# Phase tables of a state-space layer in quarters, one of them kept in DRAM for a while, and one unit moved two places in the order

## The chip, the cores and the metric

The kernel runs on one core of a Trainium2 chip. The metric is the device time of one execution in microseconds, as the median of several executions. The core has TensorE (matmuls; its weight loads are listed apart), VectorE (DVE in the rows), ScalarE (ACT), GpSimd (POOL) and SyncE (SP), which sends most DMAs here. Each engine works through its own queue in order.

## The reference

One step of a decoder layer with two parallel branches, for 1024 prompt tokens and 8 x 4 sample tokens. An RMSNorm feeds one input projection; its columns go to differential attention (four heads, a gate) and to a diagonal complex state-space layer (32 groups of 16 channels, 64 states each, a GLU, a gate); one output projection leads back to the residual stream. The part that the change touches is the state-space layer:

```python
dt = exp(log_dt); mag = exp(a_re * dt)
abar = mag * (cos(a_im * dt) + 1j * sin(a_im * dt))
bbar = ((abar - 1) / a) * b
h[l] = abar * h[l-1] + bbar @ u[l]          # per group, 64 complex states
y = Re(c @ h) + d * u
z = gelu(y); z = z * sigmoid(z @ w_glu + b_glu)
out_ssm = z * silu(gs)
```

## The kernel before

The state-space layer and the first attention head's projection come first (`first_phase`, up to about 262 us of the profiled execution); attention, the other heads and the output projection follow. In the first phase the 1024 tokens are cut into 128 chunks of 8 tokens (`NK`, `CH`). The 16 pairs of groups are handled in four *maps* m = 0 to 3 of four pairs each. For a map:

- `ssm_maps` (unit M) forms the products W (six VectorE products of 128x512, lines 573 to 578) and G (GpSimd, lines 734 and 736, three passes over 128x1152) in the tiles W, Wt and G. It also builds the block-diagonal bd and scales C on ScalarE.
- `ssm_kernel` (unit N) transposes W on TensorE into BT and multiplies G by bd into the chunk's kernel, which goes through DRAM into MT.
- `norm_u` (unit L) scales the chunk inputs U by the tokens' inverse RMS, after `u_store` (unit U) has turned them through DRAM.
- `ssm_states` (unit S) multiplies U by BT, copies the result into St (ScalarE, line 786; one buffer), rotates it by the phase table E (lines 792 to 797, VectorE and GpSimd), scans over the chunks (lines 801 and 802, VectorE), rotates back into H (lines 806 to 813).
- `ssm_out` (unit O) adds MT times U and G times H on TensorE and applies the gelu (line 837, ScalarE).

The rotation uses E = exp(i phase) for each state and chunk, tiles E_re and E_im. `phases` (unit P, line 683) makes them for *half* of the maps at a time (two maps, 8 x 128 phases per partition): on VectorE a copy, seven additions that double the filled part, the reduction to within half a turn (lines 689 to 695), then on ScalarE a sine, an absolute value and a second sine (lines 696 to 698). The two halves share one buffer each for E_re and E_im, so the second half (P1) is made only after the second map (S1) has used the first.

Statistics: the tokens' squares are summed on ScalarE (line 295), and `stats` (unit T, lines 314 to 322 with `rsqrt`, lines 176 to 183) makes inverse roots in eleven-odd small VectorE operations; the last that counts here writes `rr` (line 318). `chunk_roots` (unit R) spreads them by two matmuls, which head the queue of TensorE from then on; `spread` (unit D) stores the roots to DRAM (`xrd`, line 338) and reads them back to all partitions. The gate's weights (unit W, `stream_b`, line 214) are loaded by SP and split into a high and a low part (line 201 on ScalarE, line 204 on VectorE or GpSimd). Units C, G, J are matmul units: channel projections, twelve gate products, eighteen pieces of the first head. Unit V splits the first head's weights.

What sets the order: `UNITS` (line 47) is the order in which the units are written down. On TensorE that order is kept as it stands. The queues of the other engines, SP's among them, are ordered when the program is built, by a scheduler that takes an instruction when its inputs and buffers are free by its own estimates, and among several the one written first. At run time each queue is in order, and waits.

Buffers: tiles of one tag share a fixed number of buffers (G three, U, BT and MT two, St, X and H one, `big` with W, Wt, Z and others four). Before the maps start, `spare` lends such buffers to the twelve loads of the transposed input (`SPARE`, line 75); E_re and E_im are among those lent.

Of the kernel before, what the change touches and what calls it, by code (L numbers as in the profile page):

```python
# [9 lines left out]
F32 = mybir.dt.float32  # L10
# [3 lines left out]
OP = mybir.AluOpType  # L14
AX = mybir.AxisListType

D = 1024
# [8 lines left out]
W = 512  # L26
# [14 lines left out]
NK = S // CH  # L41
SPLITS = ((0, 352), (352, 352), (704, 352))
UC = 145
HC = 137
VW = 383

UNITS = ("M0 P0 T0 C20 C30 U0 U1 C21 R0 L0 M1 N0 C31 D0 S0 C22 L1 C32 U2 W X M2 N1 G G O0 S1 P1 L2 N2 G U3 G S2 O1 G L3 M3 G V0 N3 O2 G G S3 G V1 J J G G G Q0 J J O3 J Z0 J A0 J J B0 Z1 J Z2 J J J H0 Z3 J J H1 J J J H2 J Y0 H3 Y1 Y2 Y3").split()

GAP = 12
DUE = 5  # L50
# [21 lines left out]
NMORE = 2  # L72
LEAD = 4
PARTS = (256, 256, 512)
SPARE = {"xT": ("U", "U", "St", "H", "E_re", "E_im", "MT", "BT", "BT"),
         "xtok": ("St", "H", "BT", "BT", "MT", "MT")}
ORDER = ((0, 1, 2, 3, 4, 5, 6, 7, -1), (0, 1, 2, 3, 4, 5, -1, 6, 7))

# [65 lines left out]
class Kernel:  # L144
# [151 lines left out]

    def spare(self, name):

        sizes = {"U": (8 * UC, 2), "St": (8 * UC, 1), "H": (8 * HC, 1), "BT": (1024, 2), "MT": (1024, 2), "E_re": (8 * NK, 1),
                 "E_im": (8 * NK, 1)}  # L300
        n = self.spares.get(name, 0)
        tag = SPARE[name][n % len(SPARE[name])]
        self.spares[name] = n + 1
        return self.ss.tile([128, sizes[tag][0]], F32, name=name, tag=tag, bufs=sizes[tag][1])
# [48 lines left out]
    def first_phase(self):  # L353
        self.U, self.E, self.H, self.z_d, self.z, self.gz, self.glus = {}, {}, {}, {}, {}, {}, []
        self.zero = self.ss.tile([128, UC - NK], F32, name="zero")
        self.nc.gpsimd.memset(self.zero, 0.0)
        self.cn = self.p.tile([128, CN_W], F32, name="cn")
        nc = self.nc
        nc.sync.dma_start(self.cn, self.I["cn"])
        self.idn = self.cn[:, 0:128]  # L360
        self.A = [self.ap.tile([128, 2, NTOK], F32R, name="xt%d" % kt) for kt in range(KT)]
        self.xs = self.ap.tile([128, KT, 2, 32], F32R, name="xs")
        self.xv = self.p.tile([128, 9], F32, name="xv")
        nc.gpsimd.memset(self.xv, 1.0)
        self.spares = {}
        self.xT = []
        raw = []
        src = self.I["w_in"]
        self.sp = self.ss.tile([128, SP_W], F32, name="sp")
        for n, (n0, nn) in enumerate(SPLITS):  # L370
            parts = []
            for k0 in range(0, KT, 2):
                x = self.spare("xT")[:, 0:2 * nn].rearrange("p (k c) -> p k c", k=2)
                nc.sync.dma_start(x, self.I["xT"][128 * k0:128 * k0 + 256, n0:n0 + nn].rearrange("(k p) c -> p k c", k=2))
                parts.append((k0, 2, x))
                if n == 0 and k0 % 4 == 0:
                    i = k0 // 4
                    r = self.big("wraw")[:, 0:1024]
                    nc.sync.dma_start(r.rearrange("p (k c) -> p k c", k=4),
                                      src[512 * i:512 * i + 512, 2048:2304].rearrange("(k p) c -> p k c", k=4))  # L380
                    raw += [r[:, 0:512], r[:, 512:1024]]
            self.xT.append(parts)
            if n == 0:
                nc.sync.dma_start(self.sp, self.I["sp"])
        w = self.stream_b(2048, 1)
        self.turn = True
        self.uT = {}
        self.wu = []
        tc = self.tc
        for n in range(3):  # L390
            self.load_x(n)
            if n == 0:
                self.wu += [self.split_w(r) for r in raw]
                self.ssm_tables()
            for m in (0, 1):
                self.u_part(m, n)
        self.wu += list(w)
        for n in range(3):
            self.squares(n)
        self.gs_d = {}  # L400
        gs = None
        hs, self.w0 = self.first_head(), []
        unit = {"T": lambda i: self.stats(), "M": self.ssm_maps, "N": self.ssm_kernel, "D": lambda i: self.spread(), "R": lambda i: self.chunk_roots(), "U": self.u_store, "L": self.norm_u, "P": self.phases,
                "Z": self.load_z, "Q": lambda i: self.load_wglu(), "A": lambda i: self.lam(), "B": lambda i: self.bias(), "H": self.load_gz, "Y": self.glu, "S": self.ssm_states, "O": self.ssm_out}
        with tc.manual_schedule(engines={mybir.EngineType.PE}):
            for c in UNITS:
                if c[0] == "W":
                    self.turn = None
                    wg = list(self.stream_b(2560))
                elif c[0] == "X":  # L410
                    for kt in range(KT):
                        self.nc.scalar.activation(self.xs[:, kt, :, :], self.A[kt][:, :, S:NTOK].bitcast(F32), AF.Copy)
                    gs = self.gate(wg)
                elif c[0] == "C":
                    self.u_part(int(c[1]), int(c[2]))
                elif c[0] == "G":
                    next(gs)
                elif c[0] == "V":
                    self.turn = None
                    self.w0.append([self.split_w(r) for r in self.half_head(int(c[1]))])  # L420
                elif c[0] == "J":
                    next(hs)
                else:
                    unit[c[0]](int(c[1]))
            assert next(gs, None) is next(hs, None) is None
# [254 lines left out]
        f1, f2 = (ft[:, o:o + 128].rearrange("p (t b) -> p t b", t=16) for o in (0, 128))  # L680
        self.cmul(g, self.fins[:, 0], self.fins[:, 1], h_re, h_im, a4r, a4i, f1, f2)

    def phases(self, hf):
        nc, v, ss = self.nc, self.nc.vector, self.ss
        hs = slice(8 * hf, 8 * hf + 8)
        f = E_re = ss.tile([128, 8, NK], F32, name="E_re", tag="E_re", bufs=1)
        E_im = ss.tile([128, 8, NK], F32, name="E_im", tag="E_im", bufs=1)

        v.tensor_copy(f[:, :, 0], self.tw[:, 0, hs])
        for i in range(7):  # L690
            n = 1 << i
            v.tensor_tensor(f[:, :, n:2 * n], f[:, :, 0:n], self.tw[:, i, hs][:, :, None].to_broadcast([128, 8, n]), op=OP.add)
        magic = 1.5 * 2.0 ** 23
        v.tensor_scalar(E_im, f, magic, None, op0=OP.add)
        v.scalar_tensor_tensor(f, E_im, magic, f, op0=OP.subtract, op1=OP.subtract)
        nc.scalar.activation(E_im, f, AF.Sin, scale=-TURN)
        nc.scalar.activation(f, f, AF.Abs)
        nc.scalar.activation(E_re, f, AF.Sin, scale=-TURN, bias=self.quarter)
        self.E[hf] = E_re, E_im

    def sp_cols(self, name, m):
        a, b = SP[name]
# [68 lines left out]
    def ssm_states(self, m):  # L771
        nc, ss = self.nc, self.ss
        v, g = nc.vector, nc.gpsimd
        ts = slice(4 * m, 4 * m + 4)
        col = lambda name: self.sp_cols(name, m)
        U = self.U[m]
        G, BT, MT = self.maps[m]
        St = ss.tile([128, 2, 4, UC], F32, name="St", tag="St", bufs=1)
        for r in range(2):
            for th in range(2):  # L780
                q = (self.sc, self.tr)[th]()
                for tl in range(2):
                    t = 2 * th + tl
# [1 line left out]
                        self.mm(q[64 * g2:64 * g2 + 64, UC * tl:UC * tl + UC], BT[:, 2 * t + g2, r, :], U[:, 2 * t + g2, :], True, True)  # L785
                nc.scalar.activation(St[:, r, 2 * th:2 * th + 2, :], q[:, 0:2 * UC].rearrange("p (t k) -> p t k", t=2), AF.Copy)

        e4 = slice(4 * (m % 2), 4 * (m % 2) + 4)
        er, ei = (x[:, e4, :] for x in self.E[m // 2])
        sr, si = St[:, 0, :, 0:NK], St[:, 1, :, 0:NK]  # L790
        X = ss.tile([128, 3, 4, NK], F32, name="X", tag="X", bufs=1)
        v.tensor_tensor(X[:, 0], er, sr, op=OP.mult)
# [10 lines left out]
        H = ss.tile([128, 8, HC], F32, name="H", tag="H", bufs=1)  # L803
# [680 lines left out]
```

## Time and profile before

| | |
|---|---|
| median of 3 runs | 672.67 us (672.23 to 678.18) |
| the profiled execution | 677.08 us, its span 675.1 us |
| TensorE matmul busy in that span | 602.6 us (89%) |
| VectorE busy | 454.8 us (67%) |
| ScalarE busy | 320.1 us (47%) |
| GpSimd busy | 135.5 us (20%) |
| mean granted TensorE clock | 0.946 of full speed |

The rows that follow the change come from views of this one execution. Times are microseconds from the start of the span. A row of the timeline has the start, the time from the first start to the last end of instructions that were merged, engine, line of the program, operation, what is written from what, its shape and how many; in brackets the time that the engine sat idle before it and what ended that. A row of waits has the waiting engine, tile and line, the releaser, the total, the number and the longest. An engine that waits for a port inside an instruction counts as busy.

### The profile page before, as it was taken

To read this page: it belongs to the slowest core of one execution; us is meant where nothing else is said; L and a number is where in the kernel's file an instruction comes from. 1 tells how busy PE (TensorE), PEld (TensorE's weight loads), DVE (VectorE), ACT (ScalarE), POOL (GpSimd) and SP (SyncE) were. 2 spreads that over 40 slices of the span, in tenths; PEclk is the share of its full clock that TensorE was granted. 3 is DMA by queue.
4 is the path that set the end of the run, shared out by engine and by line. 5 is a ranking of instruction groups with operands and counts; after the bars stand their busy time and mean duration, and the time that the engine had idled before them with its cause. 6 is when DMAs were issued, how large, how long until landed. Compare 5 with 4: busy or idle time off the path is not lost.

```text
span 675.1 us, 11321 instructions
## 1 busy us (share of the span) xinstructions
PE 602.6 (89%) x3696; PEld 508.5 (75%) x3696; DVE 454.8 (67%) x1455; ACT 320.1 (47%) x798; POOL 135.5 (20%) x117
## 2 busy tenths in 40 slices
PE   5898867819999999897989999989999969999997
PEld 4897866819999989665757778767787748887775
DVE  5988968692624433787979899669876899832111
ACT  6893442613055333463747666556645566421000
POOL 0336785471412233000011000011000120001000
PEclk9997879859999999896999999999999988999999
DMA  9788553314155636433244300144100366233221
GB/s 308 255 214 151 134 149 97 118 52 133 54 179 167 192 106 193 146 102 103 70 127 122 88 24 25 48 120 138 39 25 17 88 199 202 89 105 125 82 84 50
DMA packets 90712, 79.65 MB, mean 118 GB/s; under 512 B 10365, under 2 KB 78558, under 8 KB 90654
## 3 DMA queue, kind: packets, MB, share of 16 engines
q1 hardware_dynamic: 85950, 72.36, 36.5%
q10 hardware_dynamic: 4704, 6.57, 2.7%
q8 instruction: 29, 0.48, 0.3%
q14 instruction: 29, 0.24, 0.1%
HBM read 56.70 MB, written 22.20 MB: 117 GB/s over the span
## 4 chain that ended last, share of the span: by engine, by line
PE 50%; DVE 27%; ACT 7%; issue 6%; DMA 6%; POOL 3%; SPq 1%; POOLq 0%; ACTq 0%; DVEq 0%
PE acc L152 33%; PE sc L152 7%; PE pv L152 4%; DVE s L1132 3%; PE tr L1157 2%; PE tr L152 2%; DVE ws L204 2%; DMA wraw<-in_w_in 2%; DVE qt L1017 1%; DVE qss L906 1%; DVE H L809 1%; DVE s L1142 1%; DVE qt L1016 1%; ACT ws L201 1%; DVE kt L1020 1%
## 5 line engine op out<-in xcount | busy, mean ns | idle before, releaser
L152 PE MATMUL acc<-ws,xt 128*128 128x512 f32 (+1 forms) x960 | 207.8, 359 | 0.0
L152 PEld LDWEIGHTS acc<-ws,xt 128*128 128x128 f32 x960 | 148.6, 190 | 19.9 <-issue 2.4
L204 POOL TENSOR_TENSOR ws<-wraw,ws 128x512 fp32r<-128x512 f32 x30 | 42.9, 1436 | 371.9 <-ACT ws L201 363.6
L152 PE MATMUL acc<-xt,ws 128*128 128x352 f32 x576 | 101.6, 337 | 10.0 <-ACT ws L201 7.9
L152 PEld LDWEIGHTS acc<-xt,ws 128*128 128x128 f32 x576 | 97.1, 198 | 13.3 <-ACT ws L201 8.4
L152 PE MATMUL acc<-ws,o 128*128 128x512 f32 x336 | 84.5, 400 | 1.5 <-ACT ws L201 0.9
L152 PEld LDWEIGHTS acc<-ws,o 128*128 128x128 f32 x336 | 63.0, 192 | 15.0 <-ACT ws L201 1.3
L152 PE MATMUL sc<-kt,qt 128*128 128x256 f32 (+1 forms) x320 | 58.4, 297 | 11.3 <-DVE mn L1132 5.8
L152 PEld LDWEIGHTS sc<-kt,qt 128*128 128x128 f32 x320 | 46.7, 192 | 26.2 <-DVE mn L1132 8.6
L1137 ACT ACTIVATE s<-s,mn 128x128 f32<-128x128 f32 (+7 forms) x64 | 49.5, 774 | 31.0 <-DVE mn L1132 24.9
L201 ACT ACTIVATE ws<-wraw 128x512 fp32r<-128x512 f32 x68 | 41.4, 626 | 39.6 <-PE acc L152 15.4
L204 DVE TENSOR_TENSOR ws<-wraw,ws 128x512 fp32r<-128x512 f32 x38 | 36.9, 980 | 31.8 <-ACT ws L201 31.5
L1366 DVE TENSOR_TENSOR xres<-acc,xres 128x512 f32<-128x512 f32 x16 | 11.0, 690 | 52.7 <-PE acc L152 52.7
L152 PE MATMUL pv<-vo,wt 128*128 128x128 f32 x288 | 41.0, 285 | 0.7 <-ACT wt L1160 0.6
L152 PEld LDWEIGHTS pv<-vo,wt 128*128 128x128 f32 x288 | 36.1, 194 | 6.2 <-ACT wt L1160 5.4
L1160 ACT ACTIVATE wt<-tr 128x512 f32<-128x512 f32 (+3 forms) x48 | 22.6, 487 | 17.3 <-PE tr L1157 17.1
L1132 DVE CUSTOM_DVE_ANT_0 s<-sc,cb 128x512 f32<-128x512 f32 (+3 forms) x48 | 26.6, 553 | 5.1 <-PE sc L152 4.8
L1142 DVE SCALAR_TENSOR_TENSOR s<-s,ls 128x128 f32<-128x128 f32 (+7 forms) x32 | 27.2, 849 | 0.3
L1157 PE MATMUL tr<-cn,s 128*128 128x128 f32 x144 | 25.2, 285 | 0.7 <-ACT ot L1196 0.3
L1132 DVE CUSTOM_DVE_ANT_0 s<-sc,TB,mn 128x256 f32<-128x256 f32 (+1 forms) x56 | 24.8, 442 | 0.8
L152 PE MATMUL acc<-z,ws 128*128 128x352 f32 x144 | 23.9, 325 | 1.3 <-DVE ho L462 1.0
L152 PEld LDWEIGHTS acc<-z,ws 128*128 128x128 f32 x144 | 23.1, 188 | 1.8 <-DVE ho L462 1.3
(296 smaller groups left out, 986.5 us busy)
## 6 DMA issues: line engine op xcount, KB each, us to landing
wraw<-in_w_in SPq DMA_DIRECT2D x36, 256.0 KB, 3.2
xT<-in_xT SPq DMA_DIRECT2D x12, 352.0 KB, 7.2
xtok<-in_x SPq DMA_DIRECT2D x8, 512.0 KB, 3.8
cached<-in_cache_k SPq DMA_DIRECT2D x64, 64.0 KB, 1.8
cached<-in_cache_v SPq DMA_DIRECT2D x64, 64.0 KB, 1.9
wraw<-in_w_out SPq DMA_DIRECT2D x16, 256.0 KB, 2.9
xres<-in_x SPq DMA_DIRECT2D x16, 256.0 KB, 3.0
out_y<-xres SPq DMA_DIRECT2D x16, 256.0 KB, 2.1
```

Source lines behind the costliest of these rows:

```text
L152: self.nc.tensor.matmul(out, lhsT, rhs, start=start, stop=stop)
L201: nc.scalar.activation(hi, raw, AF.Copy)
L204: (nc.vector if self.turn else nc.gpsimd).tensor_tensor(lo, raw, hi.bitcast(F32), op=OP.subtract)
L809: v.tensor_tensor(H[0:64, g2::2, 1:NK + 1], X[ps, 0], X[ps, 2], op=OP.subtract)
L906: v.tensor_reduce(ss[0:n, 4 * i:4 * i + 4], qn[0:n, i].rearrange("p (c d) -> p c d", d=QD), axis=AX.X, op=OP.add)
L1016: v.tensor_copy(hi[ot], hi[ps].bitcast(F32))
L1132: v.tensor_tensor_reduce(out=s[:, k0 + a0:k0 + a1], in0=q[:, a0:a1], in1=bias, op0=OP.add, op1=OP.min, scale=1.0, scalar=last, accum_out=m)
L1137: nc.scalar.activation(s[:, 0:L], s[:, 0:L], AF.Exp, bias=last, scale=-1.0, accum_out=ls[:, 2 * i + c:2 * i + c + 1])
L1142: v.scalar_tensor_tensor(wv, st[1][:, 0:L], cf, wv, op0=OP.mult, op1=OP.add)
L1157: nc.tensor.transpose(q[:, 128 * b:128 * b + 128], wv[:, 128 * (b0 + b):128 * (b0 + b) + 128], self.idn)
L1160: nc.scalar.activation(wt[:, 0:128 * bn], q[:, 0:128 * bn], AF.Copy)
L1366: v.tensor_tensor(x, a, x, op=OP.add)
```

## The change

The tables are made a map at a time (4 x 128 phases), with three buffers each for E_re and E_im instead of one of twice the size. All four are made at one place in front, in the order P0, P3, P1, P2, so that ScalarE needs no second stay in the sine's table. The one for map 3 is stored to DRAM as soon as it is made, which frees its buffers for the fourth that is made; a new unit E3, `phases_back`, written down right after S0, loads it back into the buffers that map 0 has left. The products of map 3 (M3) are written down after S1, where P1 stood, instead of after L3. The input's loads borrow two buffers of G instead of E_re and E_im.

```diff
-UNITS = ("M0 P0 T0 C20 C30 U0 U1 C21 R0 L0 M1 N0 C31 D0 S0 C22 L1 C32 U2 W X M2 N1 G G O0 S1 P1 L2 N2 G U3 G S2 O1 G L3 M3 G V0 N3 O2 G G S3 G V1 J J G ...
+UNITS = ("M0 P0 P3 P1 P2 T0 C20 C30 U0 U1 C21 R0 L0 M1 N0 C31 D0 S0 E3 C22 L1 C32 U2 W X M2 N1 G G O0 S1 M3 L2 N2 G U3 G S2 O1 G L3 G V0 N3 O2 G G S3 G V1 J J G ...
-SPARE = {"xT": ("U", "U", "St", "H", "E_re", "E_im", "MT", "BT", "BT"),
+SPARE = {"xT": ("U", "U", "St", "H", "G", "G", "MT", "BT", "BT"),
...
-    def phases(self, hf):
+    def phases(self, m):
         nc, v, ss = self.nc, self.nc.vector, self.ss
-        hs = slice(8 * hf, 8 * hf + 8)
-        f = E_re = ss.tile([128, 8, NK], F32, name="E_re", tag="E_re", bufs=1)
-        E_im = ss.tile([128, 8, NK], F32, name="E_im", tag="E_im", bufs=1)
+        hs = slice(4 * m, 4 * m + 4)
+        f = E_re = ss.tile([128, 4, NK], F32, name="E_re", tag="E_re", bufs=3)
+        E_im = ss.tile([128, 4, NK], F32, name="E_im", tag="E_im", bufs=3)
...
-            v.tensor_tensor(f[:, :, n:2 * n], f[:, :, 0:n], self.tw[:, i, hs][:, :, None].to_broadcast([128, 8, n]), op=OP.add)
+            v.tensor_tensor(f[:, :, n:2 * n], f[:, :, 0:n], self.tw[:, i, hs][:, :, None].to_broadcast([128, 4, n]), op=OP.add)
...
-        self.E[hf] = E_re, E_im
+        if m == 3:
+
+            self.e_d = self.dr.tile([2, 128, 4 * NK], F32, name="ed")
+            for i, x in enumerate((E_re, E_im)):
+                nc.sync.dma_start(self.e_d[i], x.rearrange("p t k -> p (t k)"))
+        else:
+            self.E[m] = E_re, E_im
+
+    def phases_back(self, m):
+        self.E[m] = []
+        for i, n in enumerate(("E_re", "E_im")):
+            x = self.ss.tile([128, 4, NK], F32, name=n, tag=n, bufs=3)
+            self.nc.sync.dma_start(x.rearrange("p t k -> p (t k)"), self.e_d[i])
+            self.E[m].append(x)
...
-        e4 = slice(4 * (m % 2), 4 * (m % 2) + 4)
-        er, ei = (x[:, e4, :] for x in self.E[m // 2])
+        er, ei = self.E[m]
```

## Rows read from the trace of the kernel before

**Rows 1.** Waits of TensorE from 28 to 180 us: total, times, longest.

```profile
PE tr L752 <- DVE W L575: 9.8, 1, 9.8
PE sc L152 <- ACT St L786: 4.4, 1, 4.4
PE tr L152 <- POOL G L736: 4.2, 1, 4.2
PE tr L152 <- DVE rr L318: 4.1, 1, 4.1
```

**Rows 2.** Busy time by stretch: from:to, length, engines, granted clock, DMA share, GB/s.

```profile
140.00:152.00 12.00, 3.17 (x24) 2.09 (x24) 11.49 (x10) 2.62 (x5) 8.38 (x5) 0.50 0.19 59
152.00:177.00 25.00, 24.96 (x188) 24.29 (x184) 11.59 (x22) 6.26 (x18) 5.53 (x7) 0.94 0.36 101
...
177.00:240.00 63.00, 61.99 (x490) 60.78 (x491) 26.46 (x31) 26.92 (x46) 19.78 (x13) 1.00 0.52 158
```

**Rows 3.** Timeline of GpSimd, first map's G: first and last of three.

```profile
44.81 2.27 POOL L734 TENSOR_TENSOR Wt<-C,P 128x1152 f32<-128x1152 f32 x1 [2.93 <-DMA C<-in_c]
...
49.40 2.64 POOL L736 TENSOR_TENSOR G<-G,Wt 128x1152 f32<-128x1152 f32 x1
```

**Rows 4.** Timeline of VectorE, first half of the tables and the statistics.

```profile
39.16 0.69 DVE L204 TENSOR_TENSOR ws<-wraw,ws 128x512 fp32r<-128x512 f32 x1 [1.38 <-ACT ws L201]
39.76 2.38 DVE L692 TENSOR_TENSOR E_re<-E_re,tw 128x8 f32<-128x8 f32 x7
42.18 0.70 DVE L694 TENSOR_SCALAR E_im<-E_re 128x1024 f32<-128x1024 f32 x1
42.91 1.22 DVE L695 SCALAR_TENSOR_TENSOR E_re<-E_im,E_re 128x1024 f32<-128x1024 f32 x1
45.78 1.33 DVE L314 TENSOR_SCALAR xv<-xv 128x9 f32<-128x9 f32 x1 [1.65 <-ACT xtok L295]
...
52.10 0.17 DVE L179 SCALAR_TENSOR_TENSOR xr<-xtmp,xr 128x9 f32<-128x9 f32 x1
...
53.13 0.29 DVE L318 TENSOR_TENSOR rr<-cn,xr 128x128 f32<-128x128 f32 x1
```

**Rows 5.** Timeline of VectorE, second half of the tables and after.

```profile
113.63 1.04 DVE L689 COPY E_re<-tw 128x8 f32<-128x8 f32 x1
...
119.50 1.23 DVE L695 SCALAR_TENSOR_TENSOR E_re<-E_im,E_re 128x1024 f32<-128x1024 f32 x1
...
126.75 0.69 DVE L792 TENSOR_TENSOR X<-E_re,St 128x512 f32<-128x512 f32 x1 [5.59 <-ACT E_re L698]
...
143.65 1.35 DVE L513 TENSOR_TENSOR U<-U,RU 128x1160 f32<-128x1160 f32 x1
```

**Rows 6.** Timeline of GpSimd, the last map's G: first and last pass.

```profile
120.82 2.26 POOL L734 TENSOR_TENSOR G<-C,P 128x1152 f32<-128x1152 f32 x1 [4.25 <-ACT C L730]
...
148.01 2.94 POOL L736 TENSOR_TENSOR G<-G,Wt 128x1152 f32<-128x1152 f32 x1
```

**Rows 7.** Timeline of ScalarE: weight splits, first states, second stay in the sine's table.

```profile
64.24 0.63 ACT L201 ACTIVATE ws<-wraw 128x512 fp32r<-128x512 f32 x1 [5.70 <-DMA wraw<-in_w_in]
...
67.94 0.46 ACT L786 ACTIVATE St<-sc 128x290 f32<-128x290 f32 x1
...
121.20 1.28 ACT L696 ACT_TABLE_LOAD   x1
122.50 1.06 ACT L696 ACTIVATE E_im<-E_re 128x1024 f32<-128x1024 f32 x1
```

**Rows 8.** Timeline of TensorE: the last of the first map's state products.

```profile
63.92 0.67 PE L152 MATMUL tr<-U,BT 128*64 128x145 f32 x8
```

**Rows 9.** Timeline of SP's queue: the roots' store and the gate's weights.

```profile
53.12 0.37 SPq L338 DMA_DIRECT2D xrd<-xr  x1
53.54 1.62 SPq L214 DMA_DIRECT2D wraw<-in_w_in  x3
```

**Rows 10.** DMA issues of the page: tile, queue, count, KB each, us to landing.

```profile
xtok<-in_x SPq DMA_DIRECT2D x8, 512.0 KB, 3.8
```

More of the change, by code (lines that the diff above doesn't have):

```diff
@@ L45 @@
 VW = 383
-UNITS = ("M0 P0 T0 C20 C30 U0 U1 C21 R0 L0 M1 N0 C31 D0 S0 C22 L1 C32 U2 W X M2 N1 G G O0 S1 P1 L2 N2 G U3 G S2 O1 G L3 M3 G V0 N3 O2 G G S3 G V1 J J G G G Q0 J J O3 J Z0 J A0 J J B0 Z1 J Z2 J J J H0 Z3 J J H1 J J J H2 J Y0 H3 Y1 Y2 Y3").split()
+UNITS = ("M0 P0 P3 P1 P2 T0 C20 C30 U0 U1 C21 R0 L0 M1 N0 C31 D0 S0 E3 C22 L1 C32 U2 W X M2 N1 G G O0 S1 M3 L2 N2 G U3 G S2 O1 G L3 G V0 N3 O2 G G S3 G V1 J J G G G Q0 J J O3 J Z0 J A0 J J B0 Z1 J Z2 J J J H0 Z3 J J H1 J J J H2 J Y0 H3 Y1 Y2 Y3").split()
 GAP = 12
@@ L297, in spare @@
     def spare(self, name):
-        sizes = {"U": (8 * UC, 2), "St": (8 * UC, 1), "H": (8 * HC, 1), "BT": (1024, 2), "MT": (1024, 2), "E_re": (8 * NK, 1),
-                 "E_im": (8 * NK, 1)}
+        sizes = {"U": (8 * UC, 2), "St": (8 * UC, 1), "H": (8 * HC, 1), "BT": (1024, 2), "MT": (1024, 2), "G": (1152, 3)}
         n = self.spares.get(name, 0)
@@ L402, in first_phase @@
         hs, self.w0 = self.first_head(), []
-        unit = {"T": lambda i: self.stats(), "M": self.ssm_maps, "N": self.ssm_kernel, "D": lambda i: self.spread(), "R": lambda i: self.chunk_roots(), "U": self.u_store, "L": self.norm_u, "P": self.phases,
+        unit = {"T": lambda i: self.stats(), "M": self.ssm_maps, "N": self.ssm_kernel, "D": lambda i: self.spread(), "R": lambda i: self.chunk_roots(), "U": self.u_store, "L": self.norm_u, "P": self.phases, "E": self.phases_back,
                 "Z": self.load_z, "Q": lambda i: self.load_wglu(), "A": lambda i: self.lam(), "B": lambda i: self.bias(), "H": self.load_gz, "Y": self.glu, "S": self.ssm_states, "O": self.ssm_out}
```

## Prediction, before the changed kernel was run

> **What bounds the kernel now.** I read the waits of TensorE first, since its order in this phase is written out by hand: an instruction there that is not ready holds all behind it. Between 28 and 180 us its four longest waits are for the last map's products (VectorE's W), for the copies of the second-last states, for GpSimd's G and for the token statistics (rr) [rows 1]. The table of busy time by stretch says what kind of place each is. From 140 to 152 us TensorE works 3.17 of 12 us while VectorE shows 11.49 and GpSimd 8.38; from 152 on it is full, 24.96 of 25 and 61.99 of 63 [rows 2]. So whatever brings forward the output products of the third map (O2, which begin at 152 us) should reach the end; whatever is won behind a wait that stays is lost.
>
> Two busy engines at 140 to 152 us would mean that one could still be relieved. The timeline denies it. GpSimd forms G in three back-to-back instructions from 44.81 to 52.04 [rows 3]; VectorE's statistics run beside them, and there the first operation on 128x9 numbers takes 1.33 us and ends at 47.11, where GpSimd's first pass ends, while such an operation after 52.04 takes 0.17 [rows 4]. VectorE and GpSimd take turns. So I laid their instructions on one line: from 37 to 152 us neither runs in only nine gaps, 6.1 us together, the first the 1.38 us ahead of the weight split at 39.16 [rows 4], the last and largest inside the 5.59 us wait at 126.75 [rows 5]. The bound up to 152 us is this pair, not either engine.
>
> The Trainium skill, SBUF — State Buffer, "Who interferes with whom", gives the rule: a VectorE instruction with two SBUF inputs contends with a GpSimd instruction that reads SBUF, and the loser "fully blocks". The trace agrees: 1.33 us beside 0.17. The rule speaks against this change: counted engine by engine, products made earlier would free TensorE's 9.8 and 4.2 us of waits, 14 in all and some 659 us; counted as a pair, moving them frees nothing by itself.
>
> **The change part by part.**
>
> *The second half of the tables leaves the middle.* It now runs on VectorE from 113.63 to 120.73 [rows 5]. Undisturbed, the first half cost 0.17 (its copy, as its neighbours) + 2.38 + 0.70 + 1.22 = 4.5 us [rows 4]; the rest of the later stretch is blocking and two gate operations. So 4.5 us of the pair's work goes. With it goes the wait for its sines, 5.59 us on VectorE [rows 5]. GpSimd fills part of it, with G until 123.08 [rows 6] and two small products; the last three of the nine gaps, 2.1 us, are what is left. Gain 6.6.
>
> *Table loads.* Two go, 1.28 us each [rows 7]. The first lies inside the 5.59 us just counted; the second stands before the output's gelu, behind which nothing of the pair waits: nothing more. The Trainium skill, ScalarE: Activation LUTs, "What ACT_TABLE_LOAD costs", puts a switch at 2.66 us, a drain of 1.38 included. Here the load begins at 121.20, takes 1.28, and the sine begins at 122.50 [rows 7]: no drain shows; with one, the gain would be 1.4 more.
>
> *The last map's products two places up.* Their work (six VectorE products, three GpSimd passes ending at 150.96 [rows 6]) is not less; it runs inside the scan chain of the second map, which it lengthens, and no longer behind that of the third. For the pair that is a swap, and O2 needs both. Two small terms remain. The scaling of the last U (1.35 us at 143.65 [rows 5]), which O2 does not need, may fall behind: 0 to 1.35, I take 1. And the third map's states are copied by ScalarE (four copies of some 0.46, as the first map's [rows 7]) only once the second map's chain has let go of their buffer; today the sines hide this. Two copies and their start come bare if the products are used up by then: 0 to 2.5, I take 1. What stands behind them in ScalarE's queue are the gate's tanh and weight splits, which have slack. These cancel.
>
> *Quarters in front.* The trace has no quarter. Its large operations halve, its small ones do not: 0.17 + (2.38 - 0.69 + 0.2) + 0.40 + 0.66, about 3.1 us, estimated from the half [rows 4]; the bounds are 2.2 (half of a half) and 4.5. Four make 12.4 where one half made 4.5: 7.9 us more for the pair between 37 and 70 us. VectorE's idle 1.38 and 1.65 us take 3.0 at most. In detail: VectorE has the port from 38.8 to 44.8, which the first two quarters fill (6.2). The third runs into GpSimd's G and gets through only at its ends; at 52.04 I leave it 2.3 us of work. The statistics stand behind it by the order list: eleven small operations, 2.2 us unblocked. rr then ends at 52.04 + 4.5 = 56.5 instead of 53.4 [rows 4]: 3.1 late. Behind rr wait TensorE's root products with all after them, and on SP's queue the store of the roots with the gate's weight loads. The fourth quarter must wait for a buffer, that of the quarter stored to DRAM; its 3.1 us fall among the second map's products, which have a few us of slack. The first scan chain starts 3.1 to 6.2 late; I take 3.6.
>
> *ScalarE, DMA, buffers.* Twelve sine and absolute passes of some 0.6 us (1.06 for twice the size [rows 7]) replace three of 1.06: 4 us more, in a stretch where ScalarE idles 5.70 us for weights [rows 7]. Store and reload are 0.5 MB each; a load of 512 KB lands in 3.8 us [rows 10]. The reload waits for the first quarter's last reader and is needed only by the fourth map; what it holds up on SP, second-half gate weights and the next map's C, is not near its use. The input's spare buffers move to G's: cover enough, since those are free until the first map.
>
> **The sum.** 6.6 + 1 - 1 - 3.6 = 3.0 us gained, before second-order shifts in the order of VectorE's and ScalarE's queues, which no row prices. The profiled execution took 677.08 (span 675.1), 4.4 above the median of 672.67; the sum is the same against either: 674.1, or **669.7** as a median. Bounds: best 6.6 + 1.35 - 0 - 0 = 8.0, or 664.7; worst 6.6 + 0 - 2.5 - 6.2 = -2.1, or 674.8.
>
> **Rivals.**
>
> *The front is hidden.* TensorE's first state products end at 64.6 [rows 8], but ScalarE copies them only from 67.94, behind weight splits: the weights, sent on SP at 53.54 right after the root store of 53.12 [rows 9], are there at 64.24 [rows 7]. If these loads now go ahead of the store, because the statistics come later in the order, this slack swallows the delay, and the fourth quarter fills gaps. Then 6.6 + 1.35 = 8.0 and shorter cold stretches after TensorE's waits: 663.5. Against it: from 54 to 70 us the pair has only two small ones of its nine gaps, so what is put in there pushes something out.
>
> *The statistics come last.* If VectorE's queue has the fourth quarter ahead of the statistics, it waits there for the DRAM store: the squares end at 45.78 [rows 4], two quarters of sines 3.6, the store 3.8 [rows 10], so 53.2; then 3.1 and 2.2: rr near 58.5 to 60, and with the weights landing 10.7 after the root store, the first scan chain 6 to 9 late. This decides once rr passes 57.0, where the delay eats what the middle gives. With 9 and the bare copies at 2.5: 6.6 - 2.5 - 9 = -4.9, **677.6**, slower. For it: the quarters all stand ahead of the statistics in the list. Against it: the fourth is held by its buffer, and the queue takes what is ready.
>
> *Nothing arrives.* The time won at 152 us is given back between 157 and 240, if head weights or the reloaded quarter come late: 672.7. Against it: TensorE is full there [rows 2], and the weight buffers are freed by its own gate products, which come earlier too.
>
> **How the numbers follow.** Main case 0.48 (own range 665 to 675), hidden front 0.22, late statistics 0.16, nothing arrives 0.14. Predicted 669.7. About 1%, 6.7 us, is what a measurement of this kernel can tell from no change: below 665.9 is faster, above 679.4 slower. Faster takes most of the hidden front and a little of the main case, 0.23; slower the far end of late statistics, 0.08; the same 0.69. The range 662.5 to 677.5 leaves out both far ends.
>
> **What would show it.** Right: the four quarters' VectorE work between 37 and 60 us; rr near 56.5; one sine load and no sine after 65; no VectorE wait for a sine past 100 us; O2 on TensorE near 149 instead of 152. Wrong: O2 at 144 or earlier (front hidden), rr past 58 (late statistics), or O2 early and TensorE idle by more than 2 us between 157 and 240. If VectorE and GpSimd together stand still for over 8 us between 37 and 149, the pair is not the bound and the sum falls with it.

## The result, and the profile after

| | before | after |
|---|---|---|
| median of the runs beside each other (18 each) | 676.85 us (672.23 to 679.82) | 669.01 us (666.09 to 672.0) |
| ratio after to before, 95% interval | | 0.9893 (0.9875 to 0.991) |
| the profiled execution, its span | 677.08, 675.1 us | 667.01, 665.0 us |
| TensorE matmul, VectorE, ScalarE, GpSimd busy | 602.6, 454.8, 320.1, 135.5 us | 598.5, 462.0, 317.1, 135.9 us |
| mean granted TensorE clock | 0.946 | 0.953 |

The changed kernel is 1.07% faster, some 7.2 us, at the edge of what was called measurable. The time forecast (669.7) is met, the gain is not: 3.0 us had been forecast, and the median of the three runs of before (672.67) lay 4 us below that of the 18.

After, busy time by stretch (from:to, length, PE, PEld, DVE, ACT, POOL, granted clock, DMA share, GB/s):

```profile
116.00:127.00 11.00, 5.41 (x53) 4.92 (x51) 10.97 (x14) 0.00 (x0) 7.83 (x6) 0.87 0.06 18
127.00:140.00 13.00, 10.00 (x58) 10.00 (x59) 10.93 (x20) 5.33 (x15) 6.71 (x8) 0.72 0.62 193
140.00:152.00 12.00, 10.79 (x91) 10.33 (x90) 7.38 (x9) 6.00 (x16) 8.16 (x8) 1.00 0.38 115
152.00:177.00 25.00, 24.93 (x185) 24.31 (x184) 14.96 (x25) 4.64 (x12) 9.28 (x9) 1.00 0.45 115
177.00:240.00 63.00, 61.76 (x490) 60.32 (x489) 25.14 (x30) 28.15 (x49) 15.68 (x9) 1.00 0.55 168
```

After, the three longest waits of TensorE from 28 to 185 us (total, times, longest):

```profile
PE sc L152 <- ACT St L798: 8.6, 1, 8.6
PE tr L152 <- ACT BT L765: 7.3, 4, 3.8
PE tr L152 <- DVE rr L317: 5.3, 1, 5.3
```

The stretch 140 to 152 us, where TensorE worked 3.17 us of 12 at a clock of 0.50 [rows 2], is now nearly full: 10.79 at 1.00. The waits for W (9.8) and G (4.2) of [rows 1] are gone. The long one is now for the copy of states St, 8.6 us, and the timeline puts it at 130 us, ahead of the second map's output products (O1). ScalarE copies these states, the third map's, as soon as GpSimd has written the last of the second map's H, the end of that map's scan chain:

```profile
129.53 0.41 ACT L798 ACTIVATE St<-sc 128x290 f32<-128x290 f32 x1 [1.33 <-POOL H L824]
```

Behind that wait TensorE has hardly a gap; 152 to 240 us stay as full as they were, so what was won before 152 us arrives.

After, TensorE's timeline: O1's first row, the gate products behind O1, the last map's W and G, O2's first row, and the gate products behind O2 (in before, these last began at 157.10):

```profile
130.00 0.82 PE L152 MATMUL sc<-U,MT 128*128 128x137 f32 x2 [8.60 <-ACT St L798]
...
135.83 7.98 PE L152 MATMUL acc<-xt,ws 128*128 128x352 f32 x48
143.65 1.03 PE L764 MATMUL tr<-cn,W 128*128 128x128 f32 x8
145.89 0.67 PE L152 MATMUL tr<-G,bd 128*32 128x128 f32 x16 [1.21 <-ACT BT L765]
146.49 0.50 PE L152 MATMUL sc<-U,MT 128*128 128x137 f32 x2
146.83 0.40 PE L152 MATMUL sc<-H,G 128*128 128x137 f32 x2
...
150.24 7.97 PE L152 MATMUL acc<-xt,ws 128*128 128x352 f32 x48
```

So the same 48 products begin 6.9 us earlier. The span is 10.1 us shorter. Matmul for matmul, TensorE's lead is still 7.0 us at 259 us and 9.6 at 289; there its longest wait for VectorE's qn, in the first head, is 1.4 us instead of 2.5. That is one profile against one, and the ratio does not carry the last 3 us.

After, VectorE: parts of the first three quarters with the statistics between them, then the start of the first scan chain, the start of the last map's W, the scaling of the third U, two scans of the second chain, and the scaling of the last U:

```profile
39.76 0.23 DVE L691 TENSOR_TENSOR E_re<-E_re,tw 128x4 f32<-128x4 f32 x2
...
39.98 2.19 DVE L691 TENSOR_TENSOR E_re<-E_re,tw 128x8 f32<-128x8 f32 x15
42.10 0.74 DVE L693 TENSOR_SCALAR E_im<-E_re 128x512 f32<-128x512 f32 x2
42.77 1.28 DVE L694 SCALAR_TENSOR_TENSOR E_re<-E_im,E_re 128x512 f32<-128x512 f32 x2
...
47.23 2.40 DVE L693 TENSOR_SCALAR E_im<-E_re 128x512 f32<-128x512 f32 x1
49.56 2.58 DVE L313 TENSOR_SCALAR xv<-xv 128x9 f32<-128x9 f32 x1
...
53.25 0.17 DVE L179 SCALAR_TENSOR_TENSOR xr<-xtmp,xr 128x9 f32<-128x9 f32 x1
53.46 0.17 DVE L180 SCALAR_TENSOR_TENSOR xtmp<-xr 128x9 f32<-128x9 f32 x1
...
54.27 0.29 DVE L317 TENSOR_TENSOR rr<-cn,xr 128x128 f32<-128x128 f32 x1
...
74.92 2.75 DVE L803 TENSOR_TENSOR X<-E_re,St 128x512 f32<-128x512 f32 x1
...
101.28 1.32 DVE L572 TENSOR_TENSOR W<-bb_re,A_re 128x512 f32<-128x512 f32 x1
...
108.72 2.29 DVE L512 TENSOR_TENSOR U<-U,RU 128x1160 f32<-128x1160 f32 x1 [1.26 <-DMA U<-ud]
...
117.53 2.88 DVE L812 TENSOR_TENSOR_SCAN X<-mag,X 128x128 f32<-128x128 f32 x1
120.34 0.39 DVE L813 TENSOR_TENSOR_SCAN St<-mag,X 128x128 f32<-128x128 f32 x1
...
147.12 1.36 DVE L512 TENSOR_TENSOR U<-U,RU 128x1160 f32<-128x1160 f32 x1
```

After, GpSimd: first pass of the second map's G, and the last map's G:

```profile
63.09 2.27 POOL L746 TENSOR_TENSOR G<-C,P 128x1152 f32<-128x1152 f32 x1 [10.56 <-ACT C L742]
...
107.53 2.25 POOL L746 TENSOR_TENSOR Wt<-C,P 128x1152 f32<-128x1152 f32 x1 [1.23 <-DVE W L577]
...
114.34 2.72 POOL L746 TENSOR_TENSOR G<-C,P 128x1152 f32<-128x1152 f32 x1
117.14 3.00 POOL L748 TENSOR_TENSOR G<-G,Wt 128x1152 f32<-128x1152 f32 x1
```

The two engines block each other as before: a scan of 128x128 takes 2.88 us beside the last pass of G (117.14 to 120.14), and the next, of the same size, 0.39 right after it. The Trainium skill, SBUF — State Buffer, "Who interferes with whom", has the loser of the shared port blocked for the whole of the other's instruction; 2.88 beside 0.39 agrees.

To compare orders I laid VectorE's and GpSimd's instructions on one line for each profile, as in the forecast. Times of each kernel's one profile, in us ("neither runs" is from 37 us to O2's first matmul, gaps of over 0.1 us; "G ready" and the ends of the chains are the ends of the instructions that O2 needs; with one profile a kernel, differences below some 1 us are not read):

| kernel | first chain starts | second chain starts, ends | third chain starts, ends | last map's G ready | O2 starts, ends | neither runs |
|---|---|---|---|---|---|---|
| before | 70.4 | 100.3, 115.9 | 126.8, 139.9 | 150.9 | 152.0, 157.4 | 6.1 |
| after | 74.9 | 110.9, 129.4 | 130.8, 145.5 | 120.1 | 146.5, 150.5 | 4.8 |
| M3 alone | 71.0 | 102.3, 125.0 | 134.6, 150.2 | 115.1 | 143.9, 153.7 | 4.9 |
| tables alone | 74.9 | 106.7, 122.8 | 124.6, 142.5 | 150.3 | 151.4, 157.3 | 9.2 |

### The profile page after: what moved, and what is told of

Read it like the earlier page. It is cut to its first block, busy times and chain, and to the rows that moved or that the text cites. A ratio compares the mean times of both kernels' runs of the same rounds, so it can differ in the third digit from the quotient of the medians.

```text
span 665.0 us, 11357 instructions
## 1 busy us (share of the span) xinstructions
PE 598.5 (90%) x3696; PEld 506.3 (76%) x3696; DVE 462.0 (69%) x1475; ACT 317.1 (48%) x802; POOL 135.9 (20%) x117
## 4 chain that ended last, share of the span: by engine, by line
PE 51%; DVE 23%; DMA 10%; issue 7%; ACT 5%; POOL 2%; SPq 1%; POOLq 0%; ACTq 0%; DVEq 0%
PE acc L152 34%; PE sc L152 7%; PE pv L152 4%; DVE s L1143 3%; PE tr L1168 2%; PE tr L152 2%; DMA wraw<-in_w_out 2%; DMA ud<-uT 1%; DMA C<-in_c 1%; DVE qt L1028 1%; DVE X L812 1%; DVE qss L917 1%; DVE s L1153 1%; DVE ws L204 1%; DMA wraw<-in_w_in 1%
## 5 line engine op out<-in xcount | busy, mean ns | idle before, releaser
L152 PE MATMUL acc<-xt,ws 128*128 128x352 f32 x576 | 103.1, 341 | 10.2 <-ACT ws L201 8.2
L152 PEld LDWEIGHTS acc<-xt,ws 128*128 128x128 f32 x576 | 98.8, 201 | 13.5 <-ACT ws L201 8.4
L204 DVE TENSOR_TENSOR ws<-wraw,ws 128x512 fp32r<-128x512 f32 x38 | 33.9, 897 | 34.4 <-ACT ws L201 34.2
L476 ACT ACTIVATE acc<-gs 128x352 f32<-128x352 f32 x12 | 5.6, 465 | 53.2 <-DVE gs L475 53.2
```

The source lines that it names most:

```text
L152: self.nc.tensor.matmul(out, lhsT, rhs, start=start, stop=stop)
L204: (nc.vector if self.turn else nc.gpsimd).tensor_tensor(lo, raw, hi.bitcast(F32), op=OP.subtract)
```

## Experiments

A ratio is to the kernel before, run beside it on the same chip, with its 95% interval. Before's medians there are 675.74 us for the first four experiments, 675.25 for the early C and the first three that move GpSimd's work, and 676.68 for the last three. In the pieces of code, ... stands for what is left out.

### Either part alone

*M3 alone*: the kernel before, with M3 written down behind P1.

```diff
-... O0 S1 P1 L2 N2 G U3 G S2 O1 G L3 M3 G V0 N3 O2 ...
+... O0 S1 P1 M3 L2 N2 G U3 G S2 O1 G L3 G V0 N3 O2 ...
```

> The kernel before with one edit: the last map's products (M3) written down right after P1, two places up; tables in halves as before. Theory A (VectorE and GpSimd take turns and are the bound up to the third map's output products, O2): moving work inside the stretch frees nothing but the 2.1 us in which neither ran during the wait for the sines, and perhaps 1.3 us of slow clock at O2: 1 to 3.5 us faster than before. Theory B (what counted was the place of M3 in the queues, 9.8 and 4.2 us of TensorE's waits): 6 us or more faster, most of the 7.2 us that the whole change brought.

671.22 us, ratio 0.9931 (0.9905 to 0.9957): 4.6 us faster, between the two forecasts; the interval, 2.9 to 6.4 us, reaches into both, so the time alone does not choose. The profile says more. The third chain ends 10.3 us later and G is ready 36 us earlier, so the pair's last instruction that O2 needs ends at 150.2 instead of 150.9: for the pair it is a swap. But before, the pair's last product was G, and the kernel products and all of O2 stood behind it, 6.4 us to O2's end. Here what comes last is the second part of the third map's H, and the products that do not need it have run, these among them:

```profile
143.34 0.67 PE L152 MATMUL tr<-G,bd 128*32 128x128 f32 x16 [1.71 <-ACT BT L753]
143.94 0.50 PE L152 MATMUL sc<-U,MT 128*128 128x137 f32 x2
```

From H's end at 150.2 to O2's end at 153.7 it is 3.5 us: 2.9 of the 3.7 that O2's end gains are won there.

*Tables alone*: the changed kernel, with M3 back behind L3.

```diff
-... O0 S1 M3 L2 N2 G U3 G S2 O1 G L3 G V0 N3 O2 ...
+... O0 S1 L2 N2 G U3 G S2 O1 G L3 M3 G V0 N3 O2 ...
```

> The changed kernel with M3 back at its old place after L3: the tables in quarters, in one stay, with the round trip through DRAM. Theory A: 4.5 us of table work and 2.1 us of idling leave the middle, some 4 us come in front, M3 still runs behind the third chain and TensorE still idles before O2: 1 to 4 us faster than before. Theory B: TensorE's wait for M3's W stays, so little is won: within 1.5 us of before. Theory C (the wait for the sines, 5.6 us, was the cost): 5 us or more faster.

675.18 us, ratio 0.9995 (0.9967 to 1.0023): nothing that can be told, between 2.2 us faster and 1.6 slower. TensorE's waits of before are all there, if shorter, on its timeline:

```profile
143.23 1.09 PE L764 MATMUL tr<-cn,W 128*128 128x128 f32 x4 [5.52 <-DVE W L574]
145.47 1.09 PE L764 MATMUL tr<-cn,W 128*128 128x128 f32 x4 [1.15 <-DVE W L577]
150.40 1.11 PE L152 MATMUL tr<-G,bd 128*32 128x128 f32 x16 [3.84 <-POOL G L748]
```

The middle does give about its 6.6 us: the second chain starts 6.4 late and the third 2.1 early. But the front costs it: the first chain is 4.6 late, and gaps open in which neither engine runs, 3.2 us near 60 and 3.0 near 103, the latter inside this wait of VectorE for its states:

```profile
106.73 0.69 DVE L803 TENSOR_TENSOR X<-E_re,St 128x512 f32<-128x512 f32 x1 [4.11 <-ACT St L798]
```

And the first pass of the last G, which ran in the wait for the sines before, now runs inside the third chain (at 128.43). In the end the last G is ready 0.6 us earlier.

Put together, the two parts show what each is worth on top of the other: M3 first 0.69%, the tables after it 0.38% (2.6 us, by two ratios whose intervals just overlap; in the profiles O2 ends 3.2 earlier); the tables first nothing, M3 after them 1.0%.

### The reload later

```diff
-... D0 S0 E3 C22 ... G S2 O1 ...
+... D0 S0 C22 ... G S2 E3 O1 ...
```

> The changed kernel with the reload of the stored quarter (E3) written down after S2 instead of after S0. In the changed kernel SP stands at this reload from 74.6 to 90.4 us, and the next U's store and load behind it come 10 to 17 us later than before, so that VectorE waits 1.3 us for U ahead of the second chain. Theory A: without that stall U is there in time and weight splits come earlier: 1 to 3 us faster than the changed kernel. Rival: the pair has other work in these microseconds, and the stall is hidden: within 0.7 us of the changed kernel.

668.75 us, ratio 0.9902 (0.9872 to 0.9933), no different from after. In after the reload does hold SP's queue, as its timeline shows:

```profile
70.59 4.00 SPq L779 DMA_DIRECT2D MT<-kd  x8
90.38 0.34 SPq L710 DMA_DIRECT2D E_re<-ed  x1
...
91.29 0.38 SPq L506 DMA_DIRECT2D ud<-uT  x1
...
103.69 0.34 SPq L508 DMA_DIRECT2D U<-ud  x1
```

SP issues nothing from 74.6 to 90.4, until the first map lets its table go, and the store and load of the third U come behind it; VectorE waits 1.26 us for that U at 108.72. With the reload moved, O2 starts 0.7 earlier in the profile (145.8), less than the timing can tell.

### The statistics ahead of three quarters

```diff
-... M0 P0 P3 P1 P2 T0 ...
+... M0 P0 T0 P3 P1 P2 ...
```

> The changed kernel with the statistics (T0) written down after the first quarter, ahead of the three others. Theory A: rr is 0.5 to 1 us earlier (it was 1.1 us later than before), the quarters move behind it, the work of the pair is the same: within 1 us of the changed kernel. Rival (late statistics are what the front costs): the first scan chain starts 3 us or more earlier and the kernel is 2 us or more faster than the changed one.

669.61 us, ratio 0.9923 (0.9891 to 0.9956): not faster. rr ends at 53.3 instead of 54.6 and the first chain starts at 74.6 instead of 74.9. So the late statistics are not what holds the front.

### The second map's C with the first's

After the change the second map's C is sent by SP at 51.65, behind the stored quarter (its last part goes at 49.55), and ScalarE has it at 62.70. Before, it was sent at 51.54 and used at 58.24, so what is late is the transfer, not its start. GpSimd idles 10.56 us for it, and bd and the last two copies of St stand behind this G in ScalarE's queue. The edit loads it with the first map's C:

```diff
...
-        C = ss.tile([128, 2, 8, 16], F32, name="C", tag="kb", bufs=KB)
-        nc.sync.dma_start(C.rearrange("p i t c -> p (i t c)"), self.I["c"][m])
+        for i in ((0, 1) if m == 0 else () if m == 1 else (m,)):
+            C = ss.tile([128, 2, 8, 16], F32, name="C", tag="kb", bufs=KB)
+            nc.sync.dma_start(C.rearrange("p i t c -> p (i t c)"), self.I["c"][i])
+            self.C[i] = C
+        C = self.C[m]
```

> The changed kernel with the load of the second map's C sent together with the first map's, ahead of the store of the quarter. In the changed kernel that load lands at 62.7 us instead of 56.3, G of the second map starts at 63.1 instead of 58.6, and the first scan chain at 74.9 instead of 70.4, though the statistics are only 1.1 us later. Theory D (the store delays C on the DMA queues, and that is what the front costs): G starts before 59, the first chain 3 to 4 us earlier, 1.5 to 3 us faster than the changed kernel, no more, since only 2 to 3 us stand empty for VectorE and GpSimd in front. Rival (the table work itself is what is late): within 0.7 us of the changed kernel.

668.33 us, ratio 0.9895 (0.9857 to 0.9933): no gain. GpSimd's timeline in this kernel:

```profile
56.73 3.10 POOL L749 TENSOR_TENSOR G<-C,P 128x1152 f32<-128x1152 f32 x1 [5.84 <-ACT C L745]
62.66 2.29 POOL L749 TENSOR_TENSOR Wt<-C,P 128x1152 f32<-128x1152 f32 x1 [2.83 <-issue]
...
69.56 3.13 POOL L751 TENSOR_TENSOR G<-G,Wt 128x1152 f32<-128x1152 f32 x1
```

G starts 6.4 us earlier and ends at 72.7, where it ended before the edit (72.9). The wait for C was cover for VectorE's work; without it the passes run into that work, and the first chain starts only 1.4 us earlier.

### GpSimd's work to VectorE

If the two take turns, a pass given to VectorE costs the pair no more, and less where VectorE does it faster. If GpSimd were a second engine of its own, the pass would only lengthen VectorE's queue, busy 92 of the 103 us from 37 to 140. First the last map's G alone, then every G, then the products of the scan chains too, on the changed kernel and on the one before:

```diff
+        e = v if m == 3 else g        # only the last map's G; "e = v": every G
...
-            g.tensor_tensor(y, C[:, i, :, None, :].to_broadcast(sh),
+            e.tensor_tensor(y, C[:, i, :, None, :].to_broadcast(sh),
-        g.tensor_tensor(G, G, x, op=OP.subtract)
+        e.tensor_tensor(G, G, x, op=OP.subtract)
```

```diff
-        g.tensor_tensor(X[:, 1], ei, si, op=OP.mult)
+        v.tensor_tensor(X[:, 1], ei, si, op=OP.mult)
...
-            g.tensor_tensor(H[64:128, g2::2, 1:NK + 1], X[ps, 1], x3[ps], op=OP.add)
+            v.tensor_tensor(H[64:128, g2::2, 1:NK + 1], X[ps, 1], x3[ps], op=OP.add)
```

*The last map's G:*

> The changed kernel with the three passes of the last map's G on VectorE instead of GpSimd. Theory A (both take turns on one port, so only the sum of their times counts): a pass of this size takes 2.2 to 2.7 us on GpSimd and 1.3 on VectorE (as the scaling of U), so 3 to 4 us less for the pair: O2 on TensorE 2 to 4 us earlier, 1.5 to 4 us faster than the changed kernel. Rival E (VectorE is the fuller engine by itself, busy 50 of the 52 us from 100 on): 3.9 us more for VectorE, 2 to 4 us slower.

*Every G:*

> The changed kernel with G of all four maps on VectorE. Theory A: 12 to 15 us less for the pair between 44 and 146 us, of which TensorE can follow only in part, since from the second chain's end on it works without a gap: 5 to 10 us faster than the changed kernel. Rival E (engines by themselves): 15.6 us more for VectorE, 5 us or more slower.

*Every G and the chains:*

> As e7, and the products of the scan chains (lines 804 to 829) on VectorE too, so that GpSimd keeps only clearing, copies and weight splits. Theory A: a product of 128x512 takes 1.2 to 1.6 us on GpSimd and 0.6 on VectorE, so another 3 to 4 us less per chain: 8 to 15 us faster than the changed kernel, the rest being TensorE's own time. Rival E: VectorE has 7 us more per chain: 10 us or more slower than the changed kernel.

*The same on the kernel before:*

> The kernel before (tables in halves, M3 at its old place) with G and the products of the scan chains on VectorE, as e8 has them. Theory A (turn-taking is the bound of the kernel before too): some 25 us less for the pair between 44 and 151 us, so 6 to 12 us faster than before, and what the change adds to that is small: within 4 us of e8. Rival E (engines by themselves): VectorE gets 30 us more and the kernel is 5 us or more slower than before.

| | median | ratio to before | O2 starts, ends |
|---|---|---|---|
| last map's G | 667.04 | 0.9868 (0.9825 to 0.9911) | 141.7, 146.5 |
| every G | 664.38 | 0.9827 (0.9781 to 0.9872) | 144.5, 148.5 |
| every G and the chains | 665.87 | 0.9864 (0.9818 to 0.991) | 140.6, 144.6 |
| the same on before | 669.64 | 0.9929 (0.9902 to 0.9956) | 145.0, 151.2 |

In each of the four O2 ends earlier than in the kernel it starts from, by 2.0 us (every G) to 6.2 (the kernel before). By the timing only every G is clear of the changed kernel's interval (0.9875 to 0.991), and that just, and the last is clear of 1. So the rival of two engines by themselves, which had each kernel slower, is out. The sizes forecast with turn-taking were mostly missed: by the ratios 1.7 us where 1.5 to 4 was forecast, 4.5 for 5 to 10, 2.0 for 8 to 15, and 4.8 for 6 to 12. Two passes of the last map's G on VectorE:

```profile
114.93 1.35 DVE L747 TENSOR_TENSOR G<-C,P 128x1152 f32<-128x1152 f32 x1
118.58 2.23 DVE L749 TENSOR_TENSOR G<-G,Wt 128x1152 f32<-128x1152 f32 x1
```

Undisturbed it is 1.35 us against 2.25 to 3.00 on GpSimd; blocked by GpSimd's chain products it is 2.23. The gains are smaller than a sum over the passes says, and the three edits of the changed kernel can't be put in order, since their intervals overlap. The both-idle time shows where the rest goes: with every G, with the chains too, and on the kernel before, neither engine runs for 12.4 to 13.0 us where it was 4.8 and 6.1; VectorE's longer queue stands still as a whole at its waits. So with this work moved the pair is no longer all that bounds O2. In the kernel before, where G stays the last product, 16.3 us of TensorE are still lost ahead of it:

```profile
PE tr L152 <- POOL fin L815: 16.3, 1, 16.3
```

(That wait ends at 143.93, just after VectorE's last pass of G at 143.8; the releaser named is a small copy on GpSimd.)

### Together with the early C and the late reload

The edits above, on the changed kernel: every G and the chains on VectorE, and every G alone, each with C early and the reload late.

> e8 with C early (e5) and the reload late (e3). With GpSimd's work gone from the pair, SP's stall at the reload and the late C stand open, since the pair is idle for 12 us: 1 to 4 us faster than e8. Rival: what is late in front is the weights behind the root store, not C: within 1 us of e8.

> e7 (only G on VectorE) with C early and the reload late: 1 to 4 us faster than e7, for the same reason. Rival: within 1 us of e7.

The first: 659.44 us (657.33 to 662.06), ratio 0.9771 (0.9735 to 0.9806), 15.5 us faster than before, about 8 than after, and 6 than the same kernel without the two edits, where 1 to 4 was forecast (the intervals lie apart each time). O2 runs from 136.7 to 140.9. Busy time from 37 to 140 us, first of after, then of this kernel:

```profile
sum 103.00, PE 76.97 PEld 72.35 DVE 92.40 ACT 45.51 POOL 65.49; mean PE 25.66 PEld 24.12 DVE 30.80 ACT 15.17 POOL 21.83
```

```profile
sum 103.00, PE 82.19 PEld 76.17 DVE 89.94 ACT 48.76 POOL 12.35; mean PE 27.40 PEld 25.39 DVE 29.98 ACT 16.25 POOL 4.12
```

GpSimd gave up 53 us, and VectorE, which took the work over, is busy 2.5 us less: what it had shown as busy was to a large part waiting for the port.

The second missed its forecast: 668.94 us, ratio 0.99 (0.9866 to 0.9934), by its ratio 0.7% slower than the same kernel without the early C and the late reload (0.9827; the intervals just touch). Its two longest waits of TensorE:

```profile
PE sc L152 <- ACT Z L852: 8.5, 1, 8.5
PE tr L152 <- DVE rr L317: 7.4, 1, 7.4
```

rr comes at 58.3 here, 2.1 later than with every G alone: with C early, the second map's G has moved up in VectorE's queue too, and its first pass stands among the statistics, behind a wait of 2.25 us for C (at 55.53). The Z wait comes with it, but no run shows why it is that long. An edit of one place re-deals three queues: by the ratios the same two edits were worth 6 us in the one kernel and cost 5 in the other.

## Why the forecast was right and where not

**The pair as the bound: held, up to 130 us.** VectorE and GpSimd together stand still 4.8 us between 37 and 146.5, below the 8 that would have refuted it, and the pair's work moved to the faster of the two engines brought O2 forward in five of six kernels. Counting engine by engine, 14 us of TensorE's waits would have come free; 7 did. But in after the pair sets O2 by way of the second chain: its end at 129.4 frees St, O1 begins at 130.0, and from there TensorE has one gap, the 1.21 us at 145.89. H, the end of the third chain, is there at 145.5, and the first product that reads it starts only at 146.83.

The turn-taking is as the forecast read it, but the row that it put beside the rule on two SBUF inputs (1.33 us) is of an operation with one tensor input. In the kernel before, the rows that fit are these, both of two inputs, the first beside GpSimd's last pass of G and the second after it:

```profile
49.59 2.48 DVE L178 TENSOR_TENSOR xtmp<-xtmp,xv 128x9 f32<-128x9 f32 x1
...
52.51 0.17 DVE L181 TENSOR_TENSOR xtmp<-xtmp,xv 128x9 f32<-128x9 f32 x1
```

**The second half leaves the middle, 6.6: held in its place.** No sine is waited for past 100 us. In *tables alone* the stretch from the second chain's start to the third's is 8.5 us shorter than before (17.9 for 26.4). Of these 2.3 are the first pass of the last G, which has only moved behind the third chain's start; the other 6.2 are near the forecast.

**Quarters in front: the term was mis-sized, and the delay came by another way.** Estimated at 3.1 us each, 6.2 for the first two, from 38.8 on; no row shows that start, since a weight split holds VectorE until 39.85 [rows 4]. These two run from 39.76 to 44.05, with three additions of the third among them: 4.3 us, or about the lower bound of 2.2 each. The scheduler lays two quarters' chains into each other, 15 additions in 2.19 us (0.15 each), where an operation that waits for the one before follows it after 0.21 us (53.25, 53.46); the estimate had left the small additions at the half's price. So rr is at 54.6, 1.1 late, not 56.5 and 3.1 late; the third quarter does run into GpSimd's G as foreseen (0.4 us of work take 2.40 at 47.23). Yet the first chain is 4.6 late against the forecast's 3.6. It is not rr that holds it, as the run with early statistics shows. The second map's C comes late behind the stored quarter, and with it G, bd and the last two copies of St. But C cannot be the whole of it, as its early load shows, which brings the chain forward by 1.4 us only: the fourth quarter, the scaling of the second U and two weight splits lie in the same stretch, and from 63 us to the chain's start the pair has no gap left. How the 4.6 divide between them stays open.

**The last map's products as a swap worth nothing: this is the step that failed.** The sum stopped at the pair's end, and TensorE still had its kernel products and O2 to do behind it. With M3 moved alone it is a swap for the pair (150.2 for 150.9), and the gain lies behind the pair's end. With G last, TensorE took 6.4 us from there, at a granted clock of 0.70, after it had idled 9.8 and 4.2 us [rows 1]; with H last it takes 3.5 us, at 0.81.

On top of the tables it is no swap even for the pair, whose end comes 4.8 us earlier than in *tables alone* (145.5 for 150.3). Some 3.3 of these are gaps that are gone (8.1 us ahead of the pair's end there, 4.8 in after): the last map's W and the first pass of its G run from 101.28 to 109.8, where *tables alone* has its gap of 3.0. Behind the pair's end it is 5.0 us instead of 7.0. O2's 16 pairs of matmuls take 4.0 us in after, at a granted clock of 1.00, against 5.3 in before. The scaling of the last U does fall behind O2, as the small term of 1 us had it (147.12, O2 from 146.5), and two weight splits fall behind the pair's end, which the term did not have (9.0 us of splits on the pair's line before, 7.0 after). Forecast 0, measured 4.6 us first and 6.9 on top of the tables.

**The sum.** Forecast: tables 3.0, M3 0. Measured: tables 0 alone and 2.6 with M3, M3 4.6. So the tables' term agrees once M3 is moved, as far as 2.6 can be told from 0, and the missing 4 us are M3's. Laid along the pair's line by which instruction ends last, the 6.9 us at O2's end are 5.4 of the pair (1.4 scaling, 1.9 splits, 2.5 less blocking in the scan chains, 1.2 fewer gaps up to the pair's end, less 1.6 that the maps, the statistics and the rest cost more) and 1.5 behind its end; that is one profile against one. O2 starts at 146.5; 149 was forecast, and 144 would have been the hidden front.

**Table loads, ScalarE, the reload.** The one sine load came true. "No sine after 65" is wrong, as is the end of the quarters' VectorE work by 60: the fourth quarter's additions end only at 70.4, its work on VectorE at 75.0 and its last sine at 77.8. No second load comes of it, because no other table is loaded before:

```profile
77.06 0.72 ACT L697 ACTIVATE E_re<-E_re,quarter 128x512 f32<-128x512 f32 x1
...
81.21 1.28 ACT L476 ACT_TABLE_LOAD   x1
```

"Not near its use" was wrong for what the reload holds up on SP (the third U, 1.26 us of VectorE's wait), and right for its price (below 1 us).

**The rivals.** The hidden front needs O2 at 144 or earlier: no. The late statistics need rr past 57.0: 54.6. Nothing arrives: the stretch from 152 to 240 us is as full as before, and TensorE's lead is 6.9 us at 163 and 7.0 at 259.

**The base.** The forecast was laid against a median of three runs, 672.67; over 18 runs it is 676.85. The two errors, 4 us of base and 4 of gain, cancelled in the time: that 669.7 was met is luck.

## To carry over

Where two engines are laid on one line to find the bound, follow the line past its end: what the last product releases on the next engine counts too, and an order in which the last product is needed by less of the work that follows is worth more than it saves the pair. Before trading work between VectorE and GpSimd, compare their prices for the same shape; where both read SBUF, the slower one's help may be a loss. Price a part with the rest of the change in place: here one part alone was worth nothing that could be told, and some 2.6 us with the other; and the move that is a swap by itself filled gaps that the other part had opened.

## What the hardware showed that was not expected

- A pass over 128x1152 float32 takes 1.35 us on VectorE and 2.25 to 3.00 on GpSimd, and while it lasts there, VectorE mostly stands (0.4 us of work took 2.40). With G and the chains on VectorE, C early and the reload late, the kernel is 2.3% faster than before (0.9771).
- Scans are blocked like products: 2.88 against 0.39 us. So are operations on a few elements, with two tensor inputs (2.48 against 0.17 us) and with one: 2.58 us for a TENSOR_SCALAR on 128x9 (49.56), 0.16 for one at 52.65, after GpSimd's pass.
- Small operations on VectorE that each need the one before follow each other at 0.21 us; two chains laid into each other run at 0.15 us an operation.
- After 8.6 us of idle TensorE's pairs of 128x137 took 0.66 us, and 0.40 from 134.5 on; after the 1.21 us of idle ahead of O2 they took 0.40 from 146.8 on. The granted clock was 0.72 from 127 to 140 us and 1.00 from 140 to 152.
